# Feed-forward of an encoder block: a second Strassen level for one gate-and-up product, with another order at the start of each pass

## The chip, the cores and the metric

The kernel runs on one core of a Trainium2 chip. The metric is device microseconds of one execution. Three runs of the kernel before took 2486.6 to 2487.57 us, with a median of 2487.34 us. The engines are named as in the profile: PE is TensorE, DVE is VectorE, ACT is ScalarE, POOL is GpSimd, and SP is SyncE, which only issues transfers (DMAs) here.

## What is computed

The reference is one layer of a hybrid encoder on 2048 tokens of width 1024: a mixing stage (forgetting attention and multi-scale pooling), an attention to 256 memory tokens, and a gated feed-forward block. The change touches the feed-forward block alone:

```python
hn = rmsnorm(h, g_ffn[l])
gu = jnp.einsum('bsd,df->bsf', hn, w_gate_up[l])          # 1024 -> 2 * 2816
act = jax.nn.silu(gu[..., :D_FF]) * gu[..., D_FF:]
h = h + jnp.einsum('bsf,fd->bsd', act, w_down[l])         # 2816 -> 1024
```

All inputs are fp32. To keep their precision, each operand of a product is split into two words of TensorE's 32-bit matmul type: a high word (a cast on ACT) and a low word (the operand less its high word, on DVE, `sub_hi`, line 63). `mm3` (line 66) then makes three matmuls of one: high by high, high by low, low by high.

## The kernel before

The feed-forward block works in two passes of 1024 tokens. Each pass has a gate-and-up part (`gate_up`, line 1518) and a down part (`down`, line 1576). Both are done by Strassen's method in Winograd's form, so that a two-by-two block product costs seven block products rather than eight.

In gate-and-up, the blocks are halves of the 1024 inputs (the sum index), halves of the pass's tokens (512 each), and gate against up for the 128 columns of one tile of the hidden width. There are 22 tiles t in a pass. The token side is shared by all tiles of a pass: the blocks x11, x12, x22 and the sums s1 to s4, each split into words and kept in SBUF as seven operands. The weight side is made for each tile by `weight_steps` (line 1130): the blocks b11, b21 and b22 and the sums t1 to t4, each split by ACT and DVE into a pair of words. These pairs go round a ring of eight places (`word_pair`, line 1118); a place is taken again when PE has read what stood in it.

A block product is `product` (line 1513): four steps of 128 along the sum index, three matmuls of 512 columns each, so 12 matmuls into one PSUM bank. A tile has seven of them. They accumulate in three banks, a, b and c, which are two sets that change places from tile to tile: x11 by b11 in a, copied out by ACT (line 1534, the copy that the prediction uses as a clock); x12 by b21 in c, added to that copy by DVE and put through SiLU (it is the gate's first token half); t2·s2 on top of a, copied out again (line 1566); t1·s1 in b; t3·s3 on top of a, copied out (line 1572). The two last products of a tile, t4·x22 in a and b22·s4 in b, come in the next tile's turn, after that tile's first product. So the order of PE in the turn of tile t is

```
x11(t)  t4·x22(t-1)  x12·b21(t)  b22·s4(t-1)  t2·s2(t)  t1·s1(t)  t3·s3(t)
```

The program order of PE and of SP's queue is written out by hand here (`with in_order(EN.SP)`, line 1665); the orders of ACT, DVE and POOL are worked out by a scheduler when the program is built.

Around this chain lie side jobs, which run at places (t, n) of the first pass (`early`, line 1670): n is 0 ahead of the weights of tile t, 1 behind them, 2 behind x11, 3 among the last three products. They are: the operands that don't fit earlier (`put_late`: s3, x22 and s4, loaded from DRAM; the other four lie in slabs, `SLABS`, line 1056); the last four tiles of 128 tokens, which are normed and turned by PE (`late_tile`, line 1464; 8 transposes each, in banks 6 and 7); and the sums of the down weights (`load_down`, `down_sums`, lines 1482 to 1501: four subtractions of 128x512 on POOL for each pair of tiles, and four stores), which the down part loads again.

The down part has 77 steps of 12 matmuls; `next_ops` (line 1681) makes the second pass's token operands at steps 20, 34, 48 and 62 of the first pass's down part. In the second pass there are no side jobs in gate-and-up.

Of the kernel before, what the change touches and what calls it, by code (L numbers as in the profile page):

```python
# [16 lines left out]
P = 128  # L17
# [24 lines left out]
def block_kernel(ctx: ExitStack, tc: tile.TileContext, x, xT, memT, cols, rows, w_qkvf, w_p, w_pool, w_out,  # L42
# [1013 lines left out]
    SLABS = ("x11", "x12", "s2", "s1")  # L1056

    NK = NF // 2
    wsum = [{f"t{n}": dr.tile([P, FT], F32, name=f"wt{n}k{k}") for n in range(1, 5)} for k in range(NK)]
# [3 lines left out]
    late_d = {op: [dr.tile([P, FT], F32, name=f"{op}d{j}") for j in range(4)] for op in ("s3", "s4")}  # L1063
# [66 lines left out]
    def weight_steps(raw, w, tie=()):  # L1130
# [8 lines left out]

        sub = lambda o, p_, q_: dve.tensor_tensor(out=o, in0=p_, in1=q_, op=ALU.subtract)  # L1140
        put("b11", b[0, 0])
        put("b21", b[1, 0])
# [4 lines left out]
        sub(t2, b[1, 1], t1)  # L1147
        put("t2", t2)
# [5 lines left out]
        sub(b[1, 0], b[1, 0], t2)  # L1154
        put("t4", b[1, 0])
# [3 lines left out]
    def weight_ops(raw, tie=()):  # L1159
        w = {}  # L1160
        for _ in weight_steps(raw, w, tie):
            pass
        return w
# [270 lines left out]
    with hps, ExitStack() as c0:  # L1434
# [3 lines left out]
        temp = lambda n: fb.tile([P, FT], F32, tag="t", name=n, bufs=14)[:]  # L1438
        bank = lambda n: fps.tile([P, FT], F32, tag=f"bk{n}", name=f"bk{n}", bufs=1)[:]
        OPS = ("x11", "x12", "s2", "s1", "s3", "s4", "x22")  # L1440

        def late_ops():

            for op in ("s4", "s3", "x22"):
                ops[op] = [tuple(fb.tile([P, FT], F32R, tag=f"{op}{c}{j}", name=f"{op}{c}{j}", bufs=1)[:]
                                 for c in "hl") for j in range(4)]

        def load_late(op):

            late_raw[op] = [temp("xr") for _ in range(4)]  # L1450
            for j in range(4):
                sp.dma_start(late_raw[op][j], hTd[1][j + 4] if op == "x22" else late_d[op][j][:])
# [3 lines left out]
        def put_late(op):  # L1456
            for j in range(4):
                hi, lo = ops[op][j]
                needs(act.copy(hi, late_raw[op][j]), *(emptied[:1] if op in ("x22", "s3") else ()))
                sub_hi(lo, late_raw[op][j], hi)  # L1460

        late_raw = {}

        def late_tile(i):

            halves = [temp("h2") for _ in range(2)]
            ms = fb.tile([P, 2], F32, tag="fms", name="fms", bufs=2)
            for a, hv in enumerate(halves):
                sp.dma_start(hv, h2d[i][:, a * FT:(a + 1) * FT])
                act.activation(bank(6 + a), hv, AF.Square, scale=1.0 / 32.0, accum_out=ms[:, a:a + 1])  # L1470
            pool.tensor_tensor(out=ms[:, 0:1], in0=ms[:, 0:1], in1=ms[:, 1:2], op=ALU.add)
            r = fb.tile([P, 1], F32, tag="fr", name="fr", bufs=2)
            rsqrt(r[:], ms[:, 0:1])
            for hv in halves:
                act.activation(hv, hv, AF.Copy, scale=r[:])
            def turn_(a):
                turn_normed(i, 4 * a, halves[a], bank(6 + a).rearrange("p (k t) -> p k t", k=4),
                            fb.tile([P, 4, P], F32, tag="hst", name="hst", bufs=1))

            return turn_  # L1480

        def down_sums(k):

            raw = down_raw.pop(k)
            b11, b12, b21, b22 = (raw[:, n] for n in range(4))
            sub = lambda o, p_, q_: pool.tensor_tensor(out=o, in0=p_, in1=q_, op=ALU.subtract)
            t3 = temp("t3")
            sub(t3, b22, b12)
            sub(b12, b12, b11)
            sub(b22, b22, b12)  # L1490
            sub(b21, b21, b22)
            for nm, v in (("t3", t3), ("t1", b12), ("t2", b22), ("t4", b21)):
                pool.dma_start(wsum[k][nm][:], v)
# [3 lines left out]
        def load_down(k):  # L1497
            down_raw[k] = raw = wdp.tile([P, 4, FT], F32, tag="wd", name="wdr", bufs=1)
            for c in range(2):
                sp.dma_start(raw[:, 2 * c:2 * c + 2],  # L1500
                             w_down[:, (2 * k + c) * P:(2 * k + c + 1) * P, :].rearrange("a p c -> p a c"))

        def act_sums(ps_, k, blocks, names):

            to = lambda nm: act_sum[ps_][k][nm]
            for nm in names:
                p_, q_, op = dict(s3=("a11", "a21", ALU.subtract), s1=("a21", "a22", ALU.add),
                                  s2=("s1", "a11", ALU.subtract), s4=("a12", "s2", ALU.subtract))[nm]
                blocks[nm] = temp(nm)
# [7 lines left out]

        def gate_up(ps_, between, follow, head, turned=0):

            prev = None  # L1520
            blocks = {}
            for t in range(NF + 1):
                cur = None
                if t < NF:
                    for job in between.get((t, 0), ()):
                        job()
                    w = head if t == 0 and head else weight_ops(weights_raw(t, hp, "v"), copied[4:5] if t == 5 else ())
                    for job in between.get((t, 1), ()):
                        job()
# [3 lines left out]
                    s1 = temp("s1")  # L1533
                    emptied.append(act.copy(s1, a))
                    for job in between.get((t, 2), ()):
                        job()
                else:
                    next(follow)
                if prev:
                    k, odd = divmod(prev["t"], 2)  # L1540
                    product(prev["a"], prev["w"]["t4"], "x22", False)
                    g1 = temp("g1")
                    act.activation(g1, prev["a"], AF.Silu)
# [200 lines left out]
```

## Time and profile before

| What | Value |
|---|---|
| median of three runs | 2487.34 us |
| the profiled execution | 2486.17 us |
| span of its profile, first to last instruction | 2484.4 us |
| PE busy | 2468.4 us (99%), 12899 matmuls |
| DVE busy | 1662.4 us (67%) |
| ACT busy | 1204.0 us (48%) |
| POOL busy | 745.1 us (30%) |
| gate-and-up of pass one, first copy of x11 | at 1222.90 us |
| gate-and-up of pass two, first copy of x11 | at 1855.44 us |
| granted TensorE clock | 0.999 of full speed |

How to read the rows that follow. A row of the timeline has the start in us, the length in us, the engine, the line of the kernel, the operation, what is written and read, and in brackets the idle time ahead of it and what ended it. A row of a group has the count after "x", then busy time in us and the mean of one in ns. "PEld" is the weight load that goes with each matmul. Tile names are those of the program; "bk" is a PSUM bank, "ww" a pair of the weight ring, "graw" raw gate-and-up weights, "qs", "kh", "kl" and "cb" the slabs with the token operands.

### The profile page before, as it was taken

How to read it: one execution, taken by the hardware profiler on the slowest of the kernel's cores; microseconds unless marked ns; L12 is line 12 of the kernel's file. 1: busy time of each engine (PE TensorE's matmuls, PEld its weight loads, DVE VectorE, ACT ScalarE, POOL GpSimd, SP SyncE). 2: the span in 40 equal slices, each digit the busy share in tenths (PEclk: the TensorE clock that was granted, in tenths of full speed). 3: DMA queues.
4: the chain of work that ended last, by engine and by line, in shares of the span. 5: the costliest groups of instructions: out<-in, count | busy, mean ns of one | idle time of the engine just before them, and what ended most of it. 6: DMA issues, size and time to landing. Idle time of an engine off the chain costs nothing.

```text
span 2484.4 us, 36567 instructions
## 1 busy us (share of the span) xinstructions
PE 2468.4 (99%) x12899; PEld 2109.2 (85%) x12899; DVE 1662.4 (67%) x3000; ACT 1204.0 (48%) x2308; POOL 745.1 (30%) x1012
## 2 busy tenths in 40 slices
PE   9999999999999899999999999999999999999999
PEld 8999989878888788888888888888888888888887
DVE  7444495489999855556868787667676666665554
ACT  6434341089999835445633433335443333333443
POOL 2223200045556524343135545430002222222000
PEclk9999999999999999999999999999999999999999
DMA  8665566476776443233645544467762333325666
GB/s 295 216 191 173 163 210 180 150 197 159 177 166 156 120 149 112 106 111 134 233 158 182 193 174 167 172 230 251 259 239 98 106 119 115 107 98 198 229 204 212
DMA packets 218279, 428.95 MB, mean 173 GB/s; under 512 B 25952, under 2 KB 101728, under 8 KB 207264
## 3 DMA queue, kind: packets, MB, share of 16 engines
q1 hardware_dynamic: 187920, 330.12, 42.4%
q0 software_dynamic: 30032, 96.23, 10.4%
q8 instruction: 102, 1.67, 0.3%
q14 instruction: 81, 0.66, 0.1%
q10 hardware_dynamic: 144, 0.26, 0.0%
HBM read 287.47 MB, written 134.61 MB: 170 GB/s over the span
## 4 chain that ended last, share of the span: by engine, by line
PE 83%; DVE 1%; issue 1%; POOL 1%; ACT 0%; DVEq 0%; POOLq 0%; ACTq 0%
PE bk L71 17%; PE bk L69 17%; PE bk L70 17%; PE acc L917 5%; PE sps L841 5%; PE tp L56 4%; PE mmps L69 4%; PE mmps L71 4%; PE mmps L70 4%; PE oo L69 1%; PE oo L70 1%; PE oo L71 1%; PE zp L71 1%; PE zp L69 1%; PE zp L70 1%
## 5 line engine op out<-in xcount | busy, mean ns | idle before, releaser
L64 DVE TENSOR_TENSOR ww<-draw,ww 128x512 fp32r<-128x512 f32 x308 | 209.7, 719 | 151.1 <-ACT ww L184 150.6
L184 ACT CAST ww<-draw 128x512 fp32r<-128x512 f32 x308 | 179.2, 620 | 220.9 <-PE bk L71 175.3
L64 DVE TENSOR_TENSOR ww<-graw,ww 128x512 fp32r<-128x512 f32 x220 | 174.3, 798 | 107.8 <-ACT ww L1137 107.6
L70 PE MATMUL bk<-ww,ww 128*128 128x512 f32 x619 | 240.2, 388 | 0.0
L71 PE MATMUL bk<-ww,ww 128*128 128x512 f32 x619 | 240.2, 388 | 0.0
L69 PE MATMUL bk<-ww,ww 128*128 128x512 f32 x619 | 240.1, 388 | 0.0
L1137 ACT CAST ww<-graw 128x512 fp32r<-128x512 f32 x220 | 136.0, 622 | 179.5 <-PE bk L71 164.4
L64 DVE TENSOR_TENSOR pl<-tp,ph 128x512 fp32r<-128x512 f32 (+3 forms) x298 | 177.5, 598 | 7.3 <-ACT ph L950 6.6
L69 PE MATMUL zps<-wh,xhi 128*128 128x384 f32 (+1 forms) x512 | 174.1, 340 | 0.0
L71 PE MATMUL zps<-wh,xl 128*128 128x384 f32 (+1 forms) x512 | 172.0, 336 | 0.0
L70 PE MATMUL zps<-wl,xhi 128*128 128x384 f32 (+1 forms) x512 | 171.9, 336 | 0.0
L950 ACT CAST ph<-tp 128x512 fp32r<-128x512 f32 (+3 forms) x298 | 152.7, 529 | 24.3 <-PE tp L56 22.9
L69 PE MATMUL bk<-qs,ww 128*128 128x512 f32 x352 | 137.8, 391 | 0.0
L71 PE MATMUL bk<-qs,ww 128*128 128x512 f32 x352 | 137.2, 390 | 0.1
L70 PE MATMUL bk<-kh,ww 128*128 128x512 f32 x352 | 136.9, 389 | 0.0
L69 PE MATMUL bk<-kl,ww 128*128 128x512 f32 x352 | 136.9, 389 | 0.0
L70 PE MATMUL bk<-cb,ww 128*128 128x512 f32 x352 | 136.9, 389 | 0.0
L71 PE MATMUL bk<-kl,ww 128*128 128x512 f32 x352 | 136.9, 389 | 0.0
L71 PEld LDWEIGHTS bk<-ww,ww 128*128 128x128 f32 x619 | 116.2, 188 | 24.1
L70 PEld LDWEIGHTS bk<-ww,ww 128*128 128x128 f32 x619 | 116.2, 188 | 24.0
L69 PEld LDWEIGHTS bk<-ww,ww 128*128 128x128 f32 x619 | 116.2, 188 | 23.7
L1615 POOL DMA_DIRECT2D out_dram<-o x31 | 16.7, 541 | 374.9 <-DVE o L1612 373.0
(641 smaller groups left out, 7066.1 us busy)
## 6 DMA issues: line engine op xcount, KB each, us to landing
graw<-in_w_gu_dram SPq DMA_DIRECT2D x44, 1024.0 KB, 5.6
draw<-in_w_down_dram SPq DMA_DIRECT2D x66, 256.0 KB, 4.4
xl<-in_xT_dram SPq DMA_DIRECT2D x64, 256.0 KB, 5.5
wdr<-in_w_down_dram SPq DMA_DIRECT2D x22, 512.0 KB, 4.3
xrow<-in_x_dram SPq DMA_DIRECT2D x16, 512.0 KB, 4.8
vd<-cb SPq DMA_DIRECT2D x16, 512.0 KB, 3.6
kh<-qkT1h SPq DMA_DIRECT2D x16, 512.0 KB, 10.3
kl<-qkT1l SPq DMA_DIRECT2D x16, 512.0 KB, 12.3
```

What stands on the lines that cost most here:

```text
L56: return pe.transpose(out.bitcast(F32R), src, identr[:])
L64: (eng or dve).tensor_tensor(out=lo, in0=src, in1=f(hi), op=ALU.subtract)
L69: pe.matmul(ps, lhsT=sh, rhs=mh, start=first, stop=False, skip_group_check=goes_on)
L70: pe.matmul(ps, lhsT=sh, rhs=ml, start=False, stop=False, skip_group_check=goes_on)
L71: pe.matmul(ps, lhsT=sl, rhs=mh, start=False, stop=last, skip_group_check=goes_on)
L184: act.copy(hi, raw)
L841: pe.matmul(ps[:, :w], lhsT=qs[:, i * P:(i + 1) * P], rhs=kk[:, cs], start=(a == 0), stop=(a == 1))
L917: pe.matmul(acc[:m, q0 * P:], lhsT=v[:, j, :m], rhs=(pl if low else ph)[:, q0 * P:], start=state["n"] == 1, stop=state["n"] == 2 * nk)
L950: act.copy(ph[:, sl], tp[:, sl])
L1137: needs(act.copy(quad(hi), v), *(tie if nm == "t2" else ()))
L1615: pool.dma_start(out[rows_, cs], o)
```

## The change

The product x12 by b21 of an even tile and of the odd tile after it are taken together. They share x12, so they are one product of a 512-input block with 256 columns and 512 tokens, and a second Strassen level is applied to it: seven quarter products of 256 inputs, 128 columns and 256 tokens. A quarter product is two steps of three matmuls of 256 columns. Both tiles' quarters run in the turn of the odd tile, in between its other products and in three PSUM places: half of bank 7 (u), half of the odd tile's c, and both halves of the even tile's c.

- `quarter_ops` makes the token side (seven operands of 256 tokens by 256 inputs) out of x12, once for each pass; `halves_` in `weight_steps` makes the weight side for each pair, from the odd tile's raw weights and a second load of the even tile's b21 (`pair`).
- In tiles 0 and 1 of a pass, the products t1·s1, t2·s2 and t3·s3 come right behind x11. From tile 2 on, the order is the old one without x12·b21 in even turns, and with the quarters in odd ones.
- x12 is no slab any more; s3 takes its slab, x12 is loaded late, and s4 is loaded after x12's quarters have been made.
- The weights of tile t + 1 are loaded in the turn of tile t.
- The late tiles' steps are spread over four turns each, with bank 6 alone and one buffer, and their first halves are loaded twice.
- The down weights' sums are made in halves (256 columns), one in each turn, on DVE instead of POOL, behind the latest copy of x11, with one store for all four.
- The buffers of 512 columns get fixed places by kind (`SETS`) instead of a common ring of 14.

The core of the diff:

```diff
-    SLABS = ("x11", "x12", "s2", "s1")
+    SLABS = ("x11", "s3", "s2", "s1")
...
+        t4 = b[1, 0] if pair is None else b[0, 0]
+        sub(t4, b[1, 0], t2)
+        def halves_():
+            odd = b[1, 0]
+            put_half(pair, "h11", "h21")
+            both = sum_("ht")
+            sub(both[:, :2], odd[:, :2], pair[:, :2])
+            sub(both[:, 2:], odd[:, 2:], both[:, :2])
+            put_half(both, "ht1", "ht2")
+            sub(odd[:, :2], odd[:, 2:], odd[:, :2])
+            put_half(odd, "ht3", "h22")
+            sub(pair[:, 2:], pair[:, 2:], both[:, 2:])
+            put_half(pair[:, 2:], "ht4")
+        if pair is not None and not first_pair:
+            halves_()
         put("t2", t2)
...
+        if first_pair:
+            halves_()
+        put("t4", t4)
...
+        SETS = dict(s1=[0, 1], s2=[2, 3, 4], s3=[5, 6], sum=[7, 8], h2=[9], x22=[9, 3, 6, 4], again=[8, 9], o=list(range(8)))
...
+        def quarter_ops(raws, *after):
...
+            for j in range(2):
+                r0, r1 = raws[j], raws[j + 2]
+                put(first_, j, r0[:, :B])
+                put(wide[0], j, r1)
+                tt(r1[:, B:], r0[:, B:], r1[:, B:], ALU.add)
+                tt(r0[:, B:], r0[:, :B], r0[:, B:], ALU.subtract)
+                tt(r0[:, :B], r1[:, B:], r0[:, :B], ALU.subtract)
+                tt(r1[:, :B], r1[:, :B], r0[:, :B], ALU.subtract)
+                put(wide[1], j, r1)
+                put(wide[2], j, r0)
...
+            return {(0, 0): lambda: load(0), (0, 3): lambda: square(0), (1, 0): lambda: load(1),
+                    (1, 3): lambda: square(1), (2, 2): scaled_, (2, 3): lambda: turn_(1),
+                    (3, 0): lambda: load(0), (3, 2): scaled_, (3, 3): lambda: turn_(0)}
...
+            sub = lambda o, p_, q_: dve.tensor_tensor(out=o, in0=p_, in1=q_, op=ALU.subtract)
+            needs(sub(b11, b12, b11), *after)
+            sub(b12, b22, b12)
+            sub(b22, b22, b11)
             sub(b21, b21, b22)
+            pool.dma_start(wsum[k][:, :, c * B:(c + 1) * B], raw)
...
+        def quarter(ps, wop, xop, first):
+            for j in range(2):
+                cs = slice(j * P, (j + 1) * P)
+                mm3(ps, (wop[0][:, cs], wop[1][:, cs]), quarters[xop][j], first and j == 0, j == 1, not first)
...
+            def rest(cur, begins):
+                a, b, w = cur["a"], cur["b"], cur["w"]
+                if begins:
+                    product(b, w["t1"], "s1", True)
+                product(a, w["t2"], "s2", False)
+                cur["s2"] = temp("s2", "s2")
+                copied.append(act.copy(cur["s2"], a))
+                if not begins:
+                    for job in between.get((cur["t"], 3), ()):
+                        job()
+                    product(b, w["t1"], "s1", True)
+                product(a, w["t3"], "s3", False)
+                cur["s3"] = temp("s3", "s3")
+                act.copy(cur["s3"], a)
+                dve.tensor_tensor(out=cur["s3"], in0=b, in1=cur["s3"], op=ALU.add)
...
+                    now, ahead = ahead, load_weights(t + 1) if t + 1 < NF else None
...
                     product(a, w["b11"], "x11", True)
...
+                    if t < 2:
+                        rest(cur, True)
+                        jobs(3)
...
+                if odd:
+                    u, c0, c1 = bank(7)[:, :B], bank(3 * ((t + 1 + turned) % 2) + 2), c[:, B:]
+                    s0 = prev["s1"]
+                    quarter(u, w["h11"], "a11", True)
+                    quarter(c1, w["ht1"], "s1", True)
+                    quarter(c0[:, :B], w["h21"], "a12", True)
+                    add(s0[:, :B], u)
+                    add(s1[:, B:], c1)
                 if prev:
                     product(prev["a"], prev["w"]["t4"], "x22", False)
...
-                    product(c, w["b21"], "x12", True)
-                    dve.tensor_tensor(out=s1, in0=c, in1=s1, op=ALU.add)
-                    act.activation(s1, s1, AF.Silu)
+                if odd:
+                    quarter(u, w["ht2"], "s2", False)
+                    add(s1[:, :B], u)
...
                     product(prev["b"], prev["w"]["b22"], "s4", False)
...
+                if odd:
+                    quarter(c1, w["h22"], "s4", False)
+                    quarter(u, w["ht3"], "s3", False)
+                    quarter(c0[:, B:], w["ht4"], "a22", True)
+                    add(s1[:, :B], c1)
+                    add(s0[:, B:], u)
+                    add(s1[:, B:], u)
+                    add(s0, c0)
+                    for s_ in (s0, s1):
+                        act.activation(s_, s_, AF.Silu)
...
+                if cur and t > 1:
+                    rest(cur, False)
...
+            for op in ("x12", "x22"):
                 load_late(op)
...
+            early = {(0, 2): [lambda: put_late("x22")], (1, 1): [lambda: quarter_ops(late_raw["x12"]), last_op]}
             for n in range(LATE):
+                for (t, m), job in late_tile(NT - LATE + n).items():
+                    early.setdefault((2 + 4 * n + t, m), []).append(job)
+            for n in range(2 * NK - 2):
+                early.setdefault((n + 2, 0), []).append(lambda n=n: load_down(n))
+                early.setdefault((n + 2, 2), []).append(lambda n=n: down_sums(n, emptied[-1]))
...
+                between.update({50: [load_quarters], 68: [lambda: quarter_ops(late_raw["x12"])]})
```

`last_op` loads s4 and splits it; `load_quarters` loads x12 of the second pass at step 50 of the first pass's down part.

197 lines of the change are left out of this document (108 added, 89 removed).

## The prediction

> **What bounds the kernel now.** I read the profile's page first (busy time, chain), then the table of windows for the feed-forward stages, then single instructions in the timeline, and last the waits of TensorE.
>
> ```profile
> PE 2468.4 (99%) x12899; PEld 2109.2 (85%) x12899; DVE 1662.4 (67%) x3000; ACT 1204.0 (48%) x2308; POOL 745.1 (30%) x1012
> ...
> PE 83%; DVE 1%; issue 1%; POOL 1%; ACT 0%; DVEq 0%; POOLq 0%; ACTq 0%
> ...
> 1256.00:1637.00 381.00, 381.00 (x1698) 315.42 (x1697) 281.88 (x319) 145.64 (x262) 182.67 (x220) 1.00 0.50 178
> ...
> 1852.00:2265.00 413.00, 413.00 (x1824) 341.98 (x1823) 260.39 (x349) 152.41 (x265) 100.17 (x126) 1.00 0.32 111
> ...
> PE tp L56 <- DVE pl L64: 6.6, 8, 2.9
> ```
>
> TensorE (PE) carries the chain, and in the two gate-and-up passes (third and fourth row: window, length, then busy time of PE, weight loads, DVE, ACT, POOL, granted clock, DMA share) it is busy from end to end at clock 1.00. DVE is at 74% in the first pass and 63% in the second. The last row is the longest of TensorE's own waits; none in that list lies in the feed-forward. But a matmul's listed time overlaps the next one's (0.39 long, 0.23 apart, in rows below), so "busy" hides gaps below 0.2 us. The pace is the better witness: each tile of a pass copies its first product out with one ACT instruction on line 1534.
>
> ```profile
> 1222.90 0.59 ACT L1534 COPY s<-bk 128x512 f32<-128x512 f32 x1 [1.76 <-PE bk L71]
> ...
> 1236.94 0.59 ACT L1534 COPY s<-bk 128x512 f32<-128x512 f32 x1 [0.25 <-PE bk L71]
> ...
> 1621.57 0.59 ACT L1534 COPY s<-bk 128x512 f32<-128x512 f32 x1 [1.66 <-issue]
> ...
> 1855.44 0.59 ACT L1534 COPY s<-bk 128x512 f32<-128x512 f32 x1 [0.81 <-PE bk L71]
> ...
> 1869.04 0.59 ACT L1534 COPY s<-bk 128x512 f32<-128x512 f32 x1 [1.57 <-PE bk L71]
> ...
> 2249.84 0.59 ACT L1534 COPY s<-bk 128x512 f32<-128x512 f32 x1 [1.61 <-PE bk L71]
> ...
> L1106 PE MATMUL bk<-ident,h 128*128 128x128 f32 x32 | 4.8, 272 | 0.0
> ```
>
> In the second pass 20 tiles take 2249.84 - 1869.04 = 380.80 us, 19.04 each; a tile has 7 products of 12 matmuls, so one 128x512 matmul costs 19.04 / 84 = 0.2267 us and a product 2.72. Tile 0 has five products before the next copy: 1869.04 - 1855.44 = 13.60 = 5 x 2.72. There is no slack at all: PE issues at its own pace. From 1621.57 to 1855.44 lie 8 products, the 77 steps of the down product and one more product, 86 x 2.72 = 233.9, and that is what it took. The first pass takes 384.63 for its 20 tiles, 3.8 more than 380.8, which fits the 32 transposes of the late tiles (last row) at 0.12 each; and tile 0 there lost 14.04 - 13.60 = 0.4. So time can only come from fewer PE cycles, and any wait that the change adds is paid in full.
>
> **The second Strassen level.** For each pair of tiles the two products of b21 with x12 (24 matmuls of 512 columns) become seven quarter products of 2 x 3 matmuls of 256 columns: 42. The trace has 256-column matmuls, each with weights of its own, in the last instructions and in the memory attention:
>
> ```profile
> 2478.80 0.28 PE L69 MATMUL bk<-ww,ww 128*128 128x256 f32 x1
> ...
> 2480.83 0.28 PE L71 MATMUL bk<-ww,ww 128*128 128x256 f32 x1
> ...
> 902.34 0.28 PE L69 MATMUL scps<-ww,ww 128*128 128x256 f32 x1
> ...
> 903.77 0.40 PE L69 MATMUL mmps<-qs,v 128*128 128x512 f32 x1
> ...
> 944.26 0.28 PE L69 MATMUL mops<-pTh,ww 128*128 128x256 f32 x1
> ...
> 947.09 0.28 PE L69 MATMUL scps<-ww,ww 128*128 128x256 f32 x1
> ...
> L69 PEld LDWEIGHTS bk<-ww,ww 128*128 128x128 f32 x619 | 116.2, 188 | 23.7
> ```
>
> First and last rows of three runs: 17 intervals in 2.03 us (0.1194 each), 12 in 1.43 (0.1192, the change back to 512 columns included), 24 in 2.83 (0.1179). The column of durations (0.28) is latency, not cost. I take 0.1191, nearest to this operand form: 24 x 0.2267 - 42 x 0.1191 = 5.440 - 5.002 = 0.438 us a pair, and 22 pairs in the two passes give **-9.6 us** (0.1179 gives -10.7, 0.1194 gives -9.4). Weight loads last 0.188 each and start every 0.12 us there, so they overlap and don't set the pace.
>
> The Trainium skill ("TensorE: Matmul & The Clock Gate", section "Back-to-back issue gap") gives a warm gap of N / 2.4 + 2.5 ns, 109 and 216 ns here; by it a pair would save 24 x 0.2157 - 42 x 0.1092 = 0.59 us and the whole 13.0. This trace's intervals are 10 ns longer at both sizes, which weighs on 42 matmuls more than on 24; the measured ones stand.
>
> **The first two tiles of a pass.** Tiles 0 and 1 now run x11, t1·s1, t2·s2, t3·s3 one after the other. t2·s2 and t3·s3 accumulate in the same bank, and between them ACT must copy the bank out. Until now the t1·s1 product (2.72 us) lay in that place; in the new order it lies ahead of t2·s2, covering the copy of x11, and nothing covers the second copy. That is a full stop of PE, four times (two tiles, two passes). Its price, from like events:
>
> ```profile
> 1887.66 0.39 PE L71 MATMUL bk<-qs,ww 128*128 128x512 f32 x1
> ...
> 1888.08 0.59 ACT L1534 COPY s<-bk 128x512 f32<-128x512 f32 x1 [1.61 <-PE bk L71]
> ...
> 504.95 0.08 DVE L843 DVE_READ_ACCUMULATOR2_ANT mx<- 128x1 f32 x1
> ...
> 505.09 0.50 PE L841 MATMUL sps<-kh,qs 128*128 128x512 f32 x1 [0.17 <-DVE mx L843]
> ...
> 505.42 0.40 PE L841 MATMUL sps<-kl,qs 128*128 128x512 f32 x1
> ...
> 1223.90 2.18 ACT L1459 CAST s3h<-xr 128x512 fp32r<-128x512 f32 x4
> ```
>
> The copy starts 0.42 after the last matmul's start and takes 0.59; the next matmul starts some 0.06 after its releaser (504.95 + 0.08 to 505.09), and the interval after such a start is 0.33 in place of 0.23. So 0.42 + 0.59 + 0.06 - 0.23 + 0.10 = 0.94, four times 3.8; with 0.1 each for an ACT that is in the middle of a cast, **+4.2 us** (bounds 3.4, without the stretched interval, and 5.8, with a whole cast ahead of each copy, (2.18 - 0.62) / 3 = 0.52 by the last row).
>
> **Late operands.** In tile 1 the weights' ring of eight places makes the ht4 part wait for the b22 product of tile 0; then 12 quarter matmuls (1.43) cover its cast and subtraction. Bounds 0 and 0.6 by the row below for 256 elements on DVE; I take 0.25, twice: **+0.5**. In pass one DVE also builds the x12 quarters ahead of tile 1's first quarter product, and the s4 load is queued behind that, on the same buffer.
>
> ```profile
> 1695.68 4.30 DVE L64 TENSOR_TENSOR ww<-draw,ww 128x512 fp32r<-128x512 f32 x7
> ...
> L489 DVE TENSOR_TENSOR pT<-zp,rbs x18: 414/689/702, 322.9 to 469.7; 128x512 f32<-128x512 f32 x14, 128x256 f32<-128x256 f32 x4
> ...
> 1220.00:1237.00 17.00, 16.91 (x75) 13.69 (x74) 13.18 (x22) 13.19 (x24) 0.55 (x1) 1.00 0.65 246
> ...
> 1830.00:1840.00 10.00, 10.00 (x46) 8.28 (x45) 4.08 (x7) 3.66 (x7) 0.00 (x0) 1.00 0.86 266
> ...
> L1140 DVE TENSOR_TENSOR t<-graw,t x44: 678/2078/2155, 1213.8 to 2222.5; 128x512 f32<-128x512 f32 x44
> ...
> L1486 POOL TENSOR_TENSOR wdr<-wdr x33: 1292/1305/1633, 1270.5 to 1658.8; 128x512 f32<-128x512 f32 x33
> ...
> draw<-in_w_down_dram SPq DMA_DIRECT2D x66, 256.0 KB, 4.4
> ```
>
> Back to back a 128x512 DVE instruction costs (4.30 - 0.69) / 6 = 0.60; 256 elements take at most 0.41. The quarters are 6 full and 10 half ones, some 7 us on a DVE that is 78% busy there, with some 21 us until they are wanted (x11 of tile 0 ends near 1222.7, plus seven products and two stops); the s3 operand, 4 subtractions, leaves that place. Weights of tile 1 arrive earlier, since their load now stands ahead of the others on SP, and may give back the 0.4 that tile 0 lost. Bounds -0.4 and +4 (s4 after quarters that come last, plus a load of some 4 us like the last row's, less two products); I take **0**. In pass two the quarters are made at steps 68 and on of the down product, where DVE has six tenths free (fourth row): 0. There the t1 weights are wanted one product earlier, but b21 is no longer cast ahead of them: 0.
>
> **Edits with nothing on the path.** Steady pairs: the new sums on DVE stand between PE's uses of bank 7, with 12 + 12 quarter matmuls and a product (4.1 us) and then a product and six quarter matmuls (3.4 us) to cover a 0.41 sum; ACT's in-place SiLU is read by DVE, not PE. Each pair adds on DVE one and a half subtractions of casts, four half-size sums of weights, and five half-size sums of products in place of one full: some 4 us of 38. The down weights' sums go from POOL (four of 1.3 us for each k, during which DVE instructions stretched to 2.08, fifth row) to DVE: eight of 0.41 for each k, 3.3 us a pair in pass one, while the stretching falls away; DVE ends near 80% there. Their wait on the latest bank copy holds up only the weight casts' subtractions behind them, which by the ring's order run about three products ahead of PE. If that cover were gone, each late sum costs its lateness. The late tiles keep their 32 transposes, in bank 6 alone; their second load (256 KB each) and the tie of their squares to the bank copy have a tile's time. On SP, the weights of tile t+1 now go ahead of tile t's other loads, and those for the down weights wait for one buffer behind them; the s4 load blocks SP until the quarters are made, with tile 3's weights behind it, wanted 19 us later. DMA share in pass one is 0.50.
>
> Sum: -9.6 + 4.2 + 0.5 + 0 = **-4.9 us**. The profiled execution took 2486.17 (span 2484.4), so it would take 2481.3; it lies 1.2 below the median 2487.34, which becomes **2482.4**.
>
> **Rivals.** (1) *The start of pass one is late*: quarters and s4 come after PE wants them. For it: DVE's 78% and the chained load; against: 21 us of room. 2 to 4 us more: 2484.4 to 2486.4, no measurable change. (2) *DVE becomes the pair's bound*, the end on the other side: in-order behind casts' subtractions, the sum that frees bank 7 comes after 3.4 us, and PE stops before ht3. It decides from 4.9 / 22 = 0.22 us of stop a pair; one stretched instruction (2.08) and two plain ones too many ahead of it would cost 0.5 to 1 us a pair, 11 to 22 us: 2493 to 2504. Against it: 63 to 80% busy, and POOL's long stretches are halved. (3) *Weight loads set the pace of narrow matmuls*: 42 x 0.188 = 7.90 a pair, 2.46 worse than now, 54 us: 2546 with the stops. The Trainium skill (same page and section) says that in a stream of loads and matmuls the spacing is set by both. The intervals of 0.119 under loads of 0.188 speak against it. (4) *The narrow matmul costs less than the rows show*: with no fixed part, 0.2267 / 2 = 0.113, the pair saves 0.68, 15.0 in all: 2477. The skill's gap formula above points that way; by it, 2479.0. No run of rows here is that fast. (5) *The second level gains nothing*: at 5.44 / 42 = 0.1295 a matmul it breaks even, and the stops are left: 2492.0. The step between 512 and 256 columns in the same bank could do that; the change back at 903.77 shows no such cost.
>
> **How the numbers follow.** Forecast 0.56, with an own range of 2480 to 2484; it lies so near the bound of 0.2% (5.0 us, 2482.4; about what can be told from no change) that I split it 0.40 beyond and 0.16 within. Rival 1 0.28 (within), rival 2 0.08 (0.06 slower, 0.02 within), rival 3 0.01 (slower), rival 4 0.04 (faster), rival 5 0.03 (0.02 within, 0.01 slower). Faster 0.44, same 0.48, slower 0.08. The range goes from 2479.8 (-10.7 and stops of 3.4 with nothing late: -7.3 and a little) to 2487.0, which holds the forecast and rival 1 with its bound of +4.
>
> **What would show it.** Copies of x11 of an even and the next even tile, 2 x 19.04 = 38.08 apart before, 37.64 apart in the new second pass; quarter matmuls starting every 0.119. Gaps of PE of about 0.9 us ahead of t3·s3 in tiles 0 and 1 of each pass, and none elsewhere. The forecast is wrong if pairs come closer to 38.1 or above (rivals 2, 3, 5: look at what PE waits for ahead of ht2, ht3), if those gaps are missing or twice as long, or if PE waits for s4 or the quarters near the first pass's start.

## The result and the profile after

| | before | after |
|---|---|---|
| median | 2487.43 us (4 runs, 2486.6 to 2487.57) | 2507.27 us (4 runs, 2504.48 to 2509.35) |
| ratio after / before, 95% interval | | 1.0080 (1.0062 to 1.0097) |
| the profiled execution | 2486.17 us, span 2484.4 us | 2505.92 us, span 2504.2 us |

The change makes the kernel 20 us slower. The forecast was 2482.4 us, with a range up to 2487.0.

From the page of the kernel after, busy time and the chain:

```profile
PE 2468.3 (99%) x13295; PEld 2122.9 (85%) x13295; DVE 1752.8 (70%) x3354; ACT 1229.6 (49%) x2360; POOL 677.4 (27%) x942
...
PE 79%; DVE 2%; DMA 2%; POOL 1%; issue 1%; ACT 0%; SPq 0%; POOLq 0%; DVEq 0%; ACTq 0%
```

PE's busy time is the same as before to 0.1 us (2468.4), with 396 matmuls more, many of them narrower. A matmul's listed time is latency and overlaps the next one's, so this number shows neither gain nor loss. What shows a loss is the span, 19.8 us longer, and the chain, in which PE fell from 83% to 79%.

From the table of windows of the kernel after (window, length, then busy time of PE, weight loads, DVE, ACT and POOL, granted clock, DMA share, GB/s):

```profile
1256.00:1637.00 381.00, 374.37 (x1851) 316.33 (x1850) 309.29 (x510) 155.32 (x279) 122.18 (x160) 1.00 0.52 185
1852.00:2265.00 413.00, 411.03 (x2007) 347.75 (x2007) 312.38 (x469) 160.09 (x285) 98.73 (x124) 1.00 0.35 127
```

PE now has holes in the first pass. DVE is at 81% there, as forecast ("near 80%").

From the timeline of ACT in the kernel after: the copies of x11 (line 1649 now), which served as the clock.

```profile
1223.00 0.59 ACT L1649 COPY s<-bk 128x512 f32<-128x512 f32 x1 [2.27 <-PE bk L71]
...
1632.87 0.58 ACT L1649 COPY s<-bk 128x512 f32<-128x512 f32 x1
...
1874.47 0.59 ACT L1649 COPY s<-bk 128x512 f32<-128x512 f32 x1 [1.32 <-PE bk L71]
...
1909.33 0.59 ACT L1649 COPY s<-bk 128x512 f32<-128x512 f32 x1 [1.07 <-PE bk L71]
...
1947.07 0.59 ACT L1649 COPY s<-bk 128x512 f32<-128x512 f32 x1 [1.61 <-PE bk L71]
...
2265.89 0.58 ACT L1649 COPY s<-bk 128x512 f32<-128x512 f32 x1
```

Read as segments between the same copies: tiles 0 to 21 of the first pass take 409.87 us (398.67 before), the second pass 391.42 (394.40 before), the down part between them 241.60 (233.87 before). A pair of the second pass takes 1947.07 - 1909.33 = 37.74 us, against 38.08 before: the second level works and gives 0.34 us a pair. The segments do not hold quite the same work: both tiles of the last pair now have their quarters behind the last copy, so each of the two passes holds one product less (2.72 us) and the down part more (5.0 for a pair's quarters, less the 2.72 that stood there before). With that allowed for, the first pass and its down part lose more than the second level gives.

The waits of PE in the kernel after (who waits for whom, us in total, times, longest):

```profile
PE bk L69 <- ACT s L1625: 4.4, 4, 1.8
PE bk L69 <- ACT ww L1146: 4.2, 4, 1.6
PE bk L70 <- DVE ww L64: 3.9, 1, 3.9
PE bk L69 <- ACT ww L1138: 3.1, 1, 3.1
PE bk L69 <- DVE s L1609: 1.6, 1, 1.6
```

In the kernel before, no row of the feed-forward is among the longest. To price them I took the timeline of PE and, for each matmul, the time from its start to the next start, less 0.2267 us for 512 columns and 0.1193 for 256. What is left over is the loss; it takes in what follows a stop, too.

```profile
1228.02 0.39 PE L71 MATMUL bk<-qs,ww 128*128 128x512 f32 x1
1229.08 0.50 PE L69 MATMUL bk<-kl,ww 128*128 128x512 f32 x1 [0.68 <-ACT s L1625]
...
1231.71 0.39 PE L71 MATMUL bk<-kl,ww 128*128 128x512 f32 x1
1235.17 0.50 PE L69 MATMUL bk<-qs,ww 128*128 128x512 f32 x1 [3.07 <-ACT ww L1138]
...
1236.73 0.63 PE L69 MATMUL bk<-qs,ww 128*128 128x512 f32 x1
1237.16 0.63 PE L70 MATMUL bk<-kh,ww 128*128 128x512 f32 x1
...
1247.25 0.50 PE L69 MATMUL bk<-kl,ww 128*128 128x512 f32 x1 [1.77 <-ACT s L1625]
...
1286.30 0.39 PE L69 MATMUL bk<-x12q,ww 128*128 128x256 f32 x1 [1.57 <-DVE s L1609]
...
1321.49 0.39 PE L69 MATMUL bk<-x12q,ww 128*128 128x256 f32 x1 [0.92 <-ACT ww L1146]
...
1664.39 0.39 PE L69 MATMUL bk<-ww,ww 128*128 128x512 f32 x1
1668.66 0.50 PE L70 MATMUL bk<-ww,ww 128*128 128x512 f32 x1 [3.88 <-DVE ww L64]
```

| | place | us lost |
|---|---|---|
| A | tiles 0 and 1 of both passes, ahead of t3·s3 | 0.94, 2.03, 0.98, 1.51: 5.5 |
| B | tile 1 of pass one, ahead of and in x11 | 5.2 |
| C | tile 3, ahead of a quarter product | 1.8 |
| D | tiles 5, 9, 13, 17, ahead of the ht1 and ht2 quarters | 1.66, 1.24, 1.86, 2.39: 7.1 |
| E | first pass's down part, step 6 | 5.8 |
| | sum | 25.4 |
| | less the 0.4 that the kernel before lost in tile 0, and 22 x 0.34 | -7.9 |

That makes +17.5 us. The last matmul starts at 2498.69 after and at 2480.83 before; less the first copies (1223.00 and 1222.90) that is +17.8 measured. The remaining 1.9 us of the span's 19.8 lie behind the last matmul (5.51 us from its start to the end of the span after, 3.57 before), and not in the last transfer out: DMA traffic ends near 2501, and the span some 3 us later. So the ledger closes within 0.3 us, and it names five places and this tail.

What each one waits for is found by going back from the late instruction along its own engine's queue. From the timelines of ACT, DVE, POOL and SP of the kernel after:

```profile
1228.44 0.59 ACT L1625 COPY s<-bk 128x512 f32<-128x512 f32 x1 [3.71 <-PE bk L71]
...
1234.50 0.61 ACT L1138 CAST ww<-graw 128x512 fp32r<-128x512 f32 x1
...
1245.58 0.62 ACT L1138 CAST ww<-graw 128x512 fp32r<-128x512 f32 x1 [0.20 <-PE bk L71]
1246.10 0.61 ACT L1515 CAST x12q<-xr 128x512 fp32r<-128x512 f32 x1
1246.62 0.58 ACT L1625 COPY s<-bk 128x512 f32<-128x512 f32 x1
```

```profile
1285.83 0.42 DVE L1609 TENSOR_TENSOR s<-bk,s 128x256 f32<-128x256 f32 x1
...
1319.90 0.42 DVE L1151 TENSOR_TENSOR ht<-graw,pair 128x256 f32<-128x256 f32 x1 [3.21 <-DMA hTd<-hst]
...
1658.93 0.42 DVE L1578 TENSOR_TENSOR wdr<-wdr 128x256 f32<-128x256 f32 x1 [6.04 <-DMA wdr<-in_w_down_dram]
```

```profile
1312.90 1.30 POOL L1592 TENSOR_TENSOR s<-s,s 128x512 f32<-128x512 f32 x1
1314.50 0.56 POOL L1593 DMA_DIRECT2D as4k1p<-s  x1 [0.30 <-POOL s L1592]
1315.06 0.77 POOL L1111 DMA_DIRECT2D hTd<-hst  x1
```

```profile
1649.93 0.43 SPq L1766 DMA_DIRECT2D draw<-in_w_down_dram  x1
1654.29 1.15 SPq L1570 DMA_DIRECT2D wdr<-in_w_down_dram  x2
1667.44 0.34 SPq L1765 DMA_DIRECT2D draw<-act12b  x1
...
SPq L1570 <- DMA wt<-wdr: 61.0, 8, 14.1
```

- **B.** The cast of tile 1's b11 runs at 1234.50, though ACT stood idle for 3.71 us up to 1228.44: it stood at a copy that waits for PE, and the cast was queued behind that copy, the next copy (line 1632) and the casts of x22 and of x12's quarters.
- **A.** In tile 1 the copy came at 1246.62 behind two casts that stood ahead of it in ACT's order, so the stop took 2.03 in place of 0.94.
- **C.** A half-size sum of a finished quarter (line 1609) stands on DVE behind weight subtractions and a down weights' sum; the quarter that takes its place in bank 7 waits. DVE reaches that sum 5.38 us after the start of tile 3's copy of x11.
- **D.** The `ht` sum of the halves takes a place in the ring "cm" of three buffers. Before, the late tiles' `hst` had a buffer of its own; now it is in this ring, and its store stands on POOL until 1315.06, behind a sum of the activations (line 1592) and that sum's store. DVE waits 3.21 us for that store to land, and the weights behind it are late.
- **E.** The sums of the last down weights run in the down part, as before, but in two halves, and on DVE. The load of the second half waits on SP for the single wide buffer, 3.9 us, until the store of the sums before it has landed, and goes out at 1654.29. (The 14.1 us in the row above is the same wait of the first half's load, issued at 1639.76, and PE did not stop for it.) Then DVE waits 6.04 us for the second load at the first sum, with the down part's subtractions queued behind; three of these, from 1662.34 on, took 5.07 us beside two of POOL's sums of the activations, where three took 1.89 at 1230.19. The next load of the down part, act12b, needs a buffer that these free, and is issued only at 1667.44.

### The profile page after: what moved, and what is told of

Read it like the earlier page. It is cut to its first block, busy times and chain, and to the rows that moved or that the text cites. A ratio compares the mean times of both kernels' runs of the same rounds, so it can differ in the third digit from the quotient of the medians.

```text
span 2504.2 us, 37874 instructions
## 1 busy us (share of the span) xinstructions
PE 2468.3 (99%) x13295; PEld 2122.9 (85%) x13295; DVE 1752.8 (70%) x3354; ACT 1229.6 (49%) x2360; POOL 677.4 (27%) x942
## 4 chain that ended last, share of the span: by engine, by line
PE 79%; DVE 2%; DMA 2%; POOL 1%; issue 1%; ACT 0%; SPq 0%; POOLq 0%; DVEq 0%; ACTq 0%
PE bk L71 16%; PE bk L69 16%; PE bk L70 16%; PE acc L917 5%; PE sps L841 5%; PE tp L56 4%; PE mmps L69 4%; PE mmps L71 4%; PE mmps L70 4%; PE oo L69 1%; PE oo L71 1%; PE oo L70 1%; DMA hTd<-hst 1%; PE zp L71 1%; PE zp L69 1%
## 5 line engine op out<-in xcount | busy, mean ns | idle before, releaser
L64 DVE TENSOR_TENSOR ww<-graw,ww 128x512 fp32r<-128x512 f32 x198 | 145.5, 739 | 40.4 <-ACT ww L1138 37.3
L1138 ACT CAST ww<-graw 128x512 fp32r<-128x512 f32 x176 | 108.4, 618 | 118.0 <-PE bk L71 105.0
L841 PE MATMUL sps<-kh,qs 128*128 128x512 f32 (+2 forms) x320 | 124.5, 389 | 0.8 <-DVE mx L843 0.4
```

The costliest lines, as they stand in the source:

```text
L64: (eng or dve).tensor_tensor(out=lo, in0=src, in1=f(hi), op=ALU.subtract)
L841: pe.matmul(ps[:, :w], lhsT=qs[:, i * P:(i + 1) * P], rhs=kk[:, cs], start=(a == 0), stop=(a == 1))
L1138: needs(act.copy(quad(hi), v), *(tie if nm == "t2" else ()))
```

## The experiments

The theory to be tested: the gain and the five losses are separate, and each of A, B, D and E is the price of one thing, a shared buffer or a place in an in-order queue, that can be undone alone. The first rival: DVE is too full, so that a stop that is taken away comes back elsewhere. The second: the narrow matmuls themselves cost more than forecast.

**The narrow matmuls alone**, on the kernel before. In odd tiles x12·b21 becomes 42 matmuls of 256 columns; in even tiles it is left out.

```diff
                 if cur:
-                    product(c, w["b21"], "x12", True)
+                    if t % 2:
+                        for n in range(7):
+                            for j in range(2):
...
+                                mm3(c[:, hs], (w["b21"][0][:, cs], w["b21"][1][:, cs]), (mh[:, hs], ml[:, hs]),
+                                    j == 0, j == 1)
                     dve.tensor_tensor(out=s1, in0=c, in1=s1, op=ALU.add)
```

> The kernel before, in which the odd tile's x12 by b21 product is made as 42 matmuls of 256 columns out of pieces that are there already, and the even tile's is left out (24 matmuls of 512 columns become 42 of 256; the gate of the first token half is left incomplete). Nothing else is changed: no new sums, loads, buffers or order. Both theories take the narrow matmuls for what they measured in the changed kernel's second pass (37.74 us a pair where 38.08 were), so 22 x 0.34 = 7.5 us less than before, 2480 us; by the prediction's rows it was 9.6, 2478. If the narrow matmuls themselves cost more than that, the time is above 2484.

Measured: 2495.02 us, ratio 1.0034 (1.0021 to 1.0047). A miss, and the waits of PE say why:

```profile
PE bk L69 <- ACT s L1573: 4.4, 4, 1.1
PE bk L69 <- ACT s L1579: 4.3, 5, 1.9
PE bk L69 <- ACT s L1534: 1.4, 2, 0.7
```

By the same reckoning the stops lose some 14 us more than in the kernel before; 22 x 0.34 = 7.5 is gained, and the span, 2491.8, is 7.4 longer than before's 2484.4, which fits within 1 us. Pairs of the second pass, where nothing else waits, take 37.70 us. So the second rival falls: the matmuls are as cheap as in the kernel after. What failed is the assumption that 2.72 us can be taken out of the even turns: they covered ACT's copies in the late tiles' turns and the copy of x11 in tile 0, and without any of the change's other edits the same kind of stop appears.

**The store of `hst` from another queue** (D alone): SP issues it, whose queue has no sums in it.

```diff
-def turn_normed(i, q, hn, tp, st, after=None):
+def turn_normed(i, q, hn, tp, st, after=None, store=pool):
...
-        pool.dma_start(hTd[i // 4][q:q + 4, :, i % 4 * P:(i % 4 + 1) * P].rearrange("k p t -> p k t"), st[:])
+        store.dma_start(hTd[i // 4][q:q + 4, :, i % 4 * P:(i % 4 + 1) * P].rearrange("k p t -> p k t"), st[:])
...
-                        hp.tile([P, 4, P], F32, tag="cm", name="hst", bufs=3))
+                        hp.tile([P, 4, P], F32, tag="cm", name="hst", bufs=3), None, sp)
```

> The changed kernel with one edit: the turned late tiles are stored to DRAM from SP's queue, not from POOL's, where the store stands behind POOL's sums. Theory 1 (single waits): in tiles 5, 9, 13 and 17 the sum for ht1 waits on DVE for that store to land, since it takes the same ring of three buffers, and PE then waits before the ht1 quarter; the four stops of 1.2 to 2.4 us (7.1 in all) go, and the time falls to about 2500. Rival (DVE has too much to do for each pair): the stops stay or turn up at another quarter, 2505 to 2508.

Measured: 2497.60 us, ratio 1.0045 (1.0030 to 1.0060), 0.35% or 8.7 us less than after, with intervals that don't overlap. All four stops of D are gone from the trace (7.1), and C is 0.56 instead of 1.8; A, B and E stay. The 1.9 us behind the last matmul go as well but for 0.2 (3.76 us from its start to the end of the span). D is the price of the store's place on POOL.

**A later load of the last down weights** (E alone): steps 2, 5, 12 and 15 of the down part instead of 2, 5, 6 and 9.

```diff
-                    between.update({2 + 4 * n: [lambda n=n: load_down(2 * NK - 2 + n)],
-                                    5 + 4 * n: [lambda n=n: down_sums(2 * NK - 2 + n)]})
+                    between.update({2 + 10 * n: [lambda n=n: load_down(2 * NK - 2 + n)],
+                                    5 + 10 * n: [lambda n=n: down_sums(2 * NK - 2 + n)]})
```

> The changed kernel with one edit: the last two halves of the down weights are loaded and summed at steps 2 and 5, and 12 and 15, of the first pass's down part, not at 2 and 5, and 6 and 9. Theory 1: the second load waited on SP for the one buffer, with the down part's own loads queued behind it; PE's stop of 4.0 us at step 6, and the slow clock behind it (1.8 us), go, and the time falls by some 5.8 us to about 2501. Rival (DVE waits for the load of the sums, or has too much to do): the same stop stays near steps 4 to 7, no change.

Measured: 2502.75 us, ratio 1.0069 (1.0054 to 1.0084). The stop of E is gone from the trace (one of 0.57 appears at 1842). The time alone could not have told this from after (the intervals overlap); the trace does. The queue on SP that the expectation speaks of is not what the trace shows: act12b, the next load, waits on SP for a buffer that DVE's subtractions free in both traces (11.8 us after, 6.2 here), and what is gone is DVE's own wait of 6.04. C is gone too, though this edit touches nothing ahead of tile 3.

**A cover for the second copy** (A alone): t1·s1 of tiles 0 and 1 is cut in two halves, one ahead of t2·s2 and one behind it.

```diff
-                    product(b, w["t1"], "s1", True)
+                    product(b, w["t1"], "s1", True, range(2))
...
+                if begins:
+                    product(b, w["t1"], "s1", True, range(2, 4))
                 product(a, w["t3"], "s3", False)
```

> The changed kernel with one edit: in tiles 0 and 1 of a pass the t1.s1 product is cut in two halves of six matmuls, one ahead of t2.s2 and one behind it, so that 1.36 us of PE's work lies over each copy out of the bank. Theory 1: the four stops ahead of t3.s3 (0.9, 2.0, 1.0 and 1.5 us) go but for what ACT is late by; 4 to 5 us less, about 2502 to 2503. Rival: the stops move to the next product, whose operands ACT and DVE have not made yet, above all in the first pass: 2505 to 2507.

Measured: 2504.89 us, ratio 1.0072 (1.0057 to 1.0087). The waits of PE:

```profile
PE bk L69 <- ACT ww L1138: 4.2, 1, 4.2
...
PE bk L69 <- ACT s L1625: 0.4, 1, 0.4
```

A falls from 5.5 to about 1 us, but the stop of B grows from 3.23 to 4.32: the cast of b11 comes when it comes, and the 0.94 that PE no longer loses in tile 0, it waits for there. The slow clock behind this longer stop lasts twice as long, so that B costs 7.1 us in all instead of 5.2. C is gone in this trace as well.

**Tile 1's first weights ahead of the x22 and x12 casts** (B, first try): these casts are made to wait for b11's cast of tile 1 (`firsts` holds the casts of b11, tile by tile).

```diff
-                needs(act.copy(hi, late_raw[op][j]), *(emptied[:1] if op == "x22" else ()))
+                needs(act.copy(hi, late_raw[op][j]), *(firsts[1:2] if op == "x22" else ()))
...
-            early = {(0, 2): [lambda: put_late("x22")], (1, 1): [lambda: quarter_ops(late_raw["x12"]), last_op]}
+            early = {(1, 1): [lambda: put_late("x22"), lambda: quarter_ops(late_raw["x12"], firsts[1]), last_op]}
```

> The changed kernel with one edit: ACT's casts for the x22 operand and for the x12 quarters of the first pass come only behind the cast of tile 1's first weights (b11); the x22 job moves from tile 0 to tile 1 for that. Theory 1: PE's stop of 3.2 us ahead of tile 1's x11, and the slow clock behind it (5.2 us in all), go, since the weights are in SBUF long before; about 2502. Rival (DVE has no room in these 25 us): the stop comes back in tile 1 ahead of the first quarter or of t4.x22 or b22.s4, 2505 to 2508.

Measured: 2509.11 us, ratio 1.0088 (1.0074 to 1.0102): no gain. The stop of 3.2 became 1.35 and 0.84, and the quarters came late by 0.71, 0.65 and 1.03. That is the sign which the expectation gave for its rival, a DVE without room; the last run below shows that the room was there.

**The edits of D, E and A together**, the three diffs above.

> The changed kernel with the early store, the later load and the split cover together. Theory 1 (each stop has a cause of its own): the sum of the three, 7.1 + 5.8 + 4.5 by the stops of the changed kernel's trace, about 17 us less than it: 2490, ratio to before 1.001. Rival (DVE's load of a pair): less than half of the sum, 2499 or more.

Measured: 2488.31 us, ratio 1.0007 (0.9998 to 1.0016), as the sum of the three said; 18 us of the 20 are back. Left are 10.1 us in the first pass (1.1 in the kernel before), most of them B (7.1: a stop of 4.31 and a long stretch at half clock) and C (1.5). The stops come off one by one and don't return, so the first rival, a full DVE, is not what makes D, E and A.

**The same with the edit of B, first try**, all four diffs above.

> The changed kernel with the early store, the later load, the split cover and the first weights ahead. Theory 1: what is left is the narrow matmuls' gain (22 x 0.34 = 7.5 us less than before) and small stops of 2 to 3 us: 2482 to 2484, ratio 0.998 to 0.999, faster than both kernels. Rival: stops in tile 1 of the first pass keep it at 2487 or above.

Measured: 2490.99 us, ratio 1.0016 (1.0006 to 1.0025). A miss: nothing gained, and the time is the rival's. The timeline of ACT in this kernel:

```profile
1224.63 0.59 ACT L1655 COPY s<-bk 128x512 f32<-128x512 f32 x1 [2.27 <-PE bk L71]
1228.71 0.59 ACT L1629 COPY s<-bk 128x512 f32<-128x512 f32 x1 [3.49 <-PE bk L71]
1232.79 0.59 ACT L1638 COPY s<-bk 128x512 f32<-128x512 f32 x1 [3.49 <-PE bk L71]
1233.28 0.62 ACT L1140 CAST ww<-graw 128x512 fp32r<-128x512 f32 x1
```

ACT does nothing between its copies: 3.49 us idle, twice. The casts of x22 and x12 are out of the way, but the two copies of tile 0 still stand ahead of b11's cast. The first try had moved the wrong neighbours.

**The three edits, with the down weights' sums back on POOL.**

```diff
-            sub = lambda o, p_, q_: dve.tensor_tensor(out=o, in0=p_, in1=q_, op=ALU.subtract)
+            sub = lambda o, p_, q_: pool.tensor_tensor(out=o, in0=p_, in1=q_, op=ALU.subtract)
             needs(sub(b11, b12, b11), *after)
```

> The changed kernel with the early store, the later load and the split cover, and the down weights' sums back on POOL (in halves, one store each, as in the change). Theory 1: DVE's sums do not hold PE up, so this is the same as the three edits alone within 2 us, or slower where POOL's sums stretch DVE's instructions. Rival (DVE's load): faster than the three edits by more than 3 us.

Measured: 2489.36 us, ratio 1.0012 (1.0003 to 1.0021), the same as with them on DVE (1.0007) within the intervals. B is the same 4.31; C is 1.1 instead of 1.5. The sums' move to DVE is not where the time went.

**The three edits, with tile 1's first weights ahead of tile 0's copies** (B, second try). In the order of ACT, b11's cast now comes ahead of the copy of s2, and t2's ahead of the copy of s3 (`firsts` holds the casts by name). For this the first weight steps of tile 1 are written in tile 0's turn, ahead of the copies that wait for them (`steps1`).

```diff
                 copied.append(act.copy(cur["s2"], a))
+                if begins and head and cur["t"] == 0:
+                    needs(copied[-1], firsts["b11"][1])
...
-                act.copy(cur["s3"], a)
+                s3c = act.copy(cur["s3"], a)
+                if begins and head and cur["t"] == 0:
+                    needs(s3c, firsts["t2"][1])
...
-                    jobs(2)
+                    if t == 0 and head:
+                        w1 = {}
+                        steps1 = weight_steps(ahead[0], w1, (), ahead[1], True)
+                        for n in range(3):
+                            next(steps1)
+                            if n == 1:
+                                jobs(2)
+                    else:
+                        jobs(2)
...
-                needs(act.copy(hi, late_raw[op][j]), *(emptied[:1] if op == "x22" else ()))
+                needs(act.copy(hi, late_raw[op][j]), *(firsts["b11"][1:2] if op == "x22" else ()))
...
-            early = {(0, 2): [lambda: put_late("x22")], (1, 1): [lambda: quarter_ops(late_raw["x12"]), last_op]}
+            early = {(0, 2): [lambda: put_late("x22")], (1, 1): [lambda: quarter_ops(late_raw["x12"], firsts["t2"][1]), last_op]}
```

> Built on the kernel with three edits (early store, later load, split cover; 2488.31 us, 1.0007). Added: tile 1's first weights of pass one. Its cast of b11 on ACT and the casts and sums up to t2 come ahead of tile 0's copy of s2 and of the quarter casts, in ACT's order, by dependencies; nothing else is changed, and no work is left out. Theory (order of ACT's queue): b11 of tile 1 has landed by about 1221 us and its cast then runs in ACT's idle time before 1227; the stop of 4.31 us ahead of x11 of tile 1, the 0.68 after it and the stretch at half clock that follows go, some 5 to 7 us in all, at most 1.5 of it returns as new short stops at the quarters: 2481 to 2484 us, ratio 0.9975 to 0.999, faster than both kernels. Rival (the edit only moves the stop, as in the run with four edits, because the casts ACT and DVE owe in these 20 us are more than they can do): stops of 3 to 4 us in all stay between 1228 and 1250 us, 2487 to 2490 us. Second rival (tile 1's weights land later than ACT could use them): the copy of s2 now stands behind the load, t3's product of tile 0 stops for 2 us and more, 2488 to 2491.

Measured: 2481.44 us, ratio 0.9981 (0.9972 to 0.9990): the first theory's case, and faster than both kernels. ACT's timeline and PE's waits in the feed-forward:

```profile
1222.58 0.59 ACT L1664 COPY s<-bk 128x512 f32<-128x512 f32 x1 [2.27 <-PE bk L71]
1223.06 0.62 ACT L1140 CAST ww<-graw 128x512 fp32r<-128x512 f32 x1
...
1227.55 0.57 ACT L1629 COPY s<-bk 128x512 f32<-128x512 f32 x1
...
1234.47 0.58 ACT L1664 COPY s<-bk 128x512 f32<-128x512 f32 x1
```

```profile
PE bk L69 <- ACT s L1629: 0.7, 2, 0.5
```

The cast runs at 1223.06, 11.4 us earlier than in the kernel after, and tile 1's copy of x11 at 1234.47 instead of 1240.64. Losses in the first pass fall from 10.1 to 2.3 us, in its down part to 0.5, and in the second pass PE makes no stop. C is gone as well, without an edit of its own: the instructions ahead of that sum on DVE are the same, but DVE reaches it 3.33 us after the start of tile 3's copy of x11 instead of 5.38 (3.16 and 3.52 in the runs of A and E alone, where it was gone too).

## Why the prediction was wrong, step by step

In the profiled execution the forecast was -4.9 us; measured were +19.75 (2505.92 - 2486.17). By the prediction's own steps:

| step of the prediction | forecast | measured |
|---|---|---|
| the second Strassen level | -9.6 | -7.5 |
| stops ahead of t3·s3 (A) | +4.2 | +5.5 |
| late operands in tile 1 | +0.5 | 0 |
| start of pass one (B, and the 0.4 that tile 0 lost before) | 0 | +4.8 |
| "edits with nothing on the path" (C, D, E) | 0 | +14.7 |
| behind the last matmul | | +1.9 |

The measured column adds up to 19.4; the other 0.35 is not put to a step.

**The step that failed is "edits with nothing on the path".** It judged the side jobs by their work: so many us on DVE, so many bytes, an engine 80% full. That was right (DVE is at 81%), and it was the wrong question. The two large losses, D and E (12.9 us of the 14.7), are not work but order; only C (1.8) is a DVE that lags. The prediction named the tool of E itself, the down weights' loads that "wait for one buffer", and said of the late tiles' moved steps that they "have a tile's time". It did not follow the buffer through: who else takes a place in that ring, on which queue the store that frees it stands, and what is queued behind the instruction that waits. The edit of D shows the answer for one (a store on POOL behind the activations' sums, 7.1 us), the edit of E for the other (a load that goes out late for want of the one buffer, and a sum on DVE that waits for it with the down part's work behind it, 5.8 us).

**Start of pass one.** The price of rival 1, 2 to 4 us, was nearly right and its cause was not: the quarters and s4 were in time, and tile 1's first weights were late. The prediction expected them early, "since their load now stands ahead of the others on SP". The load was early (issued at 1210.07; in the second try of B the cast ran at 1223.06), and the runs show the cast on ACT behind copies that wait for PE. The second try of B shows it: the same load, another place in ACT's order, and the stop is gone.

**The second level.** The mechanism is right, the size is off by a quarter: 0.34 us a pair, not 0.438. Narrow matmuls start 0.1196 apart in the second pass instead of 0.1191, which is 0.02 a pair, and the rest, some 0.08, lies where the widths change, at the first wide matmuls behind each run of narrow ones. (With one run of 42 narrow matmuls a pair, in the run of narrow matmuls alone, a pair takes 37.70 us instead of 37.74.) An estimate by the gap formula of the Trainium skill ("TensorE: Matmul & The Clock Gate", "Back-to-back issue gap") would have given 0.59; no run comes near it, and here the measured interval decides.

**The stops ahead of t3·s3** have the forecast form and price, 0.94 and 0.98 where ACT is free; the two dearer ones had one or two casts ahead of the copy, the case that the upper bound of 5.8 stood for.

**Rival 2** (DVE as the pair's bound) names a time of 2493 to 2504, not far from the result, but not its mechanism: pairs of the second pass take 37.74 us without a stop. Only C, 1.8 us in one tile, is of its kind. Rival 5 would have had pairs at 38.08.

**No slack.** The prediction said that "any wait that the change adds is paid in full", but counted only the stops of A and the late operands. The run of narrow matmuls alone shows the other side: a product that is removed from PE's stream was also the cover of what ran beside it. With the waits undone the kernel takes 2481.44 us, close to the 2482.4 of the forecast. That is chance: the forecast sets a gain of 9.6 against losses of 4.7, while this kernel has a gain of 7.5 and, with most of A taken away, losses of some 3.

What stays open is what puts DVE behind in tile 3 (C), and what the last 1.9 us are. They are not scatter: from the last matmul's start to the end of the span it is 5.47 to 5.51 us in the four traces of the changed kernel with the store of `hst` on POOL, 3.76 to 3.82 in the five with it on SP, and 3.57 before. So they go with the edit of D, but no run shows how.

## What to carry to other kernels

Where PE has no slack, price a moved side job by its place and not by its work: for each one write down the buffer it takes, who frees that buffer and from which queue, and what stands behind it on its own engine. An engine that shows idle time in its timeline while a ready instruction is late has an order problem; look at what it idles for, since that instruction is the one to move behind. And when a product is taken out of the stream, list what ran beside it, because its cover goes with it.

## What the runs showed of the hardware

After the longer stops PE ran for a while at half clock. From the table of windows of the kernel after, the stretch behind the stop of 3.88 us, behind that of 3.07, and one behind a stop of 1.77:

```profile
1669.40:1672.30 2.90, 2.90 (x8) 2.29 (x7) 0.80 (x2) 1.24 (x2) 2.40 (x3) 0.50 0.96 352
1236.80:1238.80 2.00, 2.00 (x6) 1.60 (x5) 2.00 (x4) 0.54 (x1) 0.00 (x0) 0.50 0.00 0
...
1248.00:1252.00 4.00, 4.00 (x26) 3.59 (x26) 3.57 (x7) 2.73 (x5) 0.00 (x0) 1.00 0.69 234
```

The granted clock is 0.50 and a 512-column matmul starts every 0.43 us (1236.73 to 1237.16 above), and it stays so for some 3.4 us: windows of 3.30 us from 1235.60 and from 1669.10 show 0.50 throughout. That adds 1.6 to 1.9 us to a stop; behind the stop of 1.77 the clock stays at 1.00. With the three edits, behind the stop of 4.16, a window of 6.70 us from 1234.50 shows 0.50, twice as long. The Trainium skill ("TensorE: Matmul & The Clock Gate", "What's actually happening") says that the clock falls to one half after an idle window of some 3.4 us, whose phase is free. The half fits; the length does not quite: 3.07 us of idle was enough here, and in the run with the later load the clock was 0.50 for 3.30 us from 1322.30, 1.5 us behind the end of a stop of 1.46 (with one of 0.22 in between). So the length of one stop alone does not tell. A restart costs some 0.11 us beside the stop itself: the interval behind every row with 0.50 for a duration is 0.33 to 0.34 instead of 0.227.
